# The sample's two token tiles at the end of the output projection, and another order of products in the first two feed-forward units

## The chip, the cores and the metric

The kernel runs on one core of a Trainium2 chip, in one launch. The metric is the device time of an execution in microseconds (us). A core has five engines, each with an instruction queue of its own that is worked through in order: PE (TensorE, the matrix products; PEld are its weight loads), DVE (VectorE), ACT (ScalarE), POOL (GpSimd) and SP (SyncE, which here issues nearly all DMAs). They meet only through semaphores: an instruction waits at the head of its queue until what it reads is written and what it overwrites has been read.

## What is computed

One encoder layer over two inputs: a prompt of 1024 tokens and a sample of 256. A mixer (gated DeltaNet heads and differential attention heads) gives 1024 numbers per token; they go through an output projection, a residual with layer norm, a SwiGLU feed-forward and a second residual with layer norm. Cut to what matters:

```python
def hybrid_mixer(x, w_in, ...):
    h = x @ w_in
    ...
    o_a = gated_deltanet_group(qkv, z, gates, ...)       # 4 heads, scans in both directions
    o_b = diff_attention_group(dq, dk, dv, ...)          # 4 heads, two softmax maps each
    return jnp.concatenate([o_a, o_b], -1) @ w_out       # output projection, 1024 x 1024

def swiglu(x, w_gate_up, w_down):
    gate, up = jnp.split(x @ w_gate_up, 2, axis=-1)      # 2 x 2816 columns
    return (jax.nn.silu(gate) * up) @ w_down

x = layer_norm(ALPHA * x + hybrid_mixer(x, ...), ln1_g, ln1_b)
x = layer_norm(ALPHA * x + swiglu(x, w_gate_up, w_down), ln2_g, ln2_b)
```

The same layer is applied to both inputs. All is float32.

## The kernel before

A product of two float32 matrices is made from three products: each operand is split into a high part (a cast, on ACT) and a low part (operand minus high part, on DVE or POOL), and high by low, low by high and high by high are summed in PSUM. A split thus costs one ACT and one DVE or POOL instruction, and needs two buffers.

The tokens lie in ten tiles of 128: tiles 0 to 7 are the prompt, tiles 8 and 9 the sample. The program has five stages, of which the middle ones matter here.

- **phase_b** (L1068): attention and scans. Attention takes one prompt head, then the sample's heads, then the other three prompt heads (ORDER), so the sample's mixer output is in memory (tensor oT of the sample) long before the prompt's. For the last prompt head attn_finish works through a chain: ACT copies and squares the last block (tiles ao, asq, ass), POOL and DVE make the inverse root (rs_r, rs_t), DVE scales ao, PE transposes it (tile rb_ps), ACT writes tile oT (L889), SP stores it to the tensor oT (L892). Meanwhile load_wout brings the output weights in eight pieces (worw) and splits them (woh on ACT, L1154; wol on DVE, L1155).
- **phase_c** (L1159): output projection and first layer norm, a tile of 128 tokens at a time, in the order of the loop at L1189. Per tile: SP loads oraw from oT (all eight heads of these tokens, L1192) and the residual input xt (L1194), ACT and POOL split oraw into oh and ol, PE does 2 times 24 matmuls of 128x512 into om_ps, DVE adds the residual (L1206), layer_norm (L1122) runs on DVE with a POOL step, two DMAs store the result to x1s (L1143). One tile later, PE transposes it (x_ps, L1174), and ACT and DVE split it: tiles 0 to 3 into B00 and B10, tiles 4 to 7 into Braw and B11, the sample's into xs.
- **x_sums** (L1224): adds and subtracts whole blocks of the transposed prompt (a Strassen scheme: seven block products in place of eight) into T1 to T4, 40 DVE instructions and 16 ACT casts. Its temporaries t come from the pool `post`, of 11 buffers, which also gives p, u and others to the units. This pool lies in memory that phase_c has used before, so its first tile waits for all that still reads or writes there.
- **sweep_up** (L1270): the gate and up products of the feed-forward in 22 units. A unit splits blocks A11, A12, A21, A22 of the weights (pool `sp`, 7 buffers) and makes: gx_ps from B00 with A11, copied to p (L1310), and then onto the same bank B10 with A12; gs_ps, the sample's four products, from xs; gy_ps and gz_ps from T1 to T4 and B11. B10 can be added only when p has been copied. The first two units are generators run in alternation, so that their first parts stand ahead of their Strassen parts.

Nothing in the source fixes the order across engines beyond this: a scheduler reorders each engine's instructions when the program is built, from its own timing model, and picks pool buffers. The order built is the order in which the chip runs them.

Of the kernel before, what the change touches and what calls it, by code (L numbers as in the profile page):

```python
# [1158 lines left out]
def phase_c(k):  # L1159


    nc, tc, V, A = k.nc, k.tc, k.nc.vector, k.nc.scalar
    with ExitStack() as es:
        pool = lambda name, bufs: es.enter_context(tc.tile_pool(name=name, bufs=bufs, side="right"))
        op, cp = pool("c_o", 2), pool("c_x", 3)
        sm, gp = pool("c_s", 2), pool("c_gb", 1)
        gb = [gp.tile([P, DM], F32, name="ln1_" + n) for n in "gb"]

        def transposes(t, xt):
            lo = (t % 4) * P  # L1170
            for b in range(2):
                ps = k.pt.tile([P, 512], F32, tag="tp", name="x1_ps")
                for i in range(4):
                    nc.tensor.transpose(ps[:, i * P:(i + 1) * P], xt[:, (4 * b + i) * P:(4 * b + i + 1) * P], k.ident)  # L1174
                pv = ps.rearrange("p (a b) -> p a b", a=4)
                if t >= 8:
                    h, l = [x[:, 4 * b:4 * b + 4, lo:lo + P] for x in k.xs]
                elif t < 4:
                    h, l = [x[:, :, lo:lo + P] for x in k.B[b, 0]]
                else:  # L1180
                    A.copy(k.Braw[b][:, :, lo:lo + P], pv)
                    if b == 0:
                        continue
                    h, l = [x[:, :, lo:lo + P] for x in k.B[1, 1]]
                A.copy(h, pv)
                V.tensor_tensor(out=l, in0=pv, in1=f32(h), op=ALU.subtract)

        pend = []
        for t in (8, 9, 0, 1, 2, 3, 4, 5, 6, 7):  # L1189
            si, c = (1, t) if t < 8 else (0, t - 8)  # L1190
            raw = op.tile([P, KT, P], F32, tag="oraw", name="oraw")
            nc.sync.dma_start(out=raw, in_=k.S.oT[si].rearrange("k p n -> p k n")[:, :, c * P:(c + 1) * P])  # L1192
            xt = cp.tile([P, DM], F32, tag="xt", name="xt")
            nc.sync.dma_start(out=xt, in_=k.x[si][c * P:(c + 1) * P, :])  # L1194
            if t == 8:
                ln_load(k, k.ln1_g, k.ln1_b, gb)
            if t == 2:
                k.raws = [pair_raw(k, 0), pair_raw(k, 1)]
            oh = op.tile([P, KT, P], F32R, tag="oh", name="oh")
            ol = op.tile([P, KT, P], F32R, tag="ol", name="ol")  # L1200
            split_w(k, raw, oh, ol)
            for o in (0, 512):
                ps = k.pm.tile([P, 512], F32, tag="mm", name="om_ps")
                mm3(nc, ps, lambda i: oh[:, i, :], lambda i: ol[:, i, :],
                    lambda i: k.woh[:, i, o:o + 512], lambda i: k.wol[:, i, o:o + 512], KT)
                V.scalar_tensor_tensor(out=xt[:, o:o + 512], in0=xt[:, o:o + 512], scalar=ALPHA, in1=ps,  # L1206
                                       op0=ALU.mult, op1=ALU.add)
            layer_norm(k, xt, gb, sm, k.S.x1[t])
            pend.append((t, xt))
            if len(pend) > LAG:  # L1210
                transposes(*pend.pop(0))
        for p in pend:
            transposes(*p)
# [46 lines left out]
def mm7(nc, ps, s, t, n, start, stop=True, again=False):  # L1260


    seq = [(s[0], t[1], i) for i in range(n)] + [(s[0], t[0], i) for i in range(n)] + [(s[1], t[0], i) for i in range(n)]
    for j, (a, b, i) in enumerate(seq):
        m = nc.tensor.matmul(ps, lhsT=a(i), rhs=b(i), start=start and j == 0, stop=stop and j == len(seq) - 1,  # L1265
                             skip_group_check=again)
    return m


def sweep_up(k, T, release):  # L1270
# [7 lines left out]
    def split(src):  # L1278
        hi = k.sp.tile([P, 4, P], F32R, tag="sp", name="sph")
        lo = k.sp.tile([P, 4, P], F32R, tag="sp", name="spl")  # L1280
        A.copy(hi, src)  # L1281
        V.tensor_tensor(out=lo, in0=src, in1=f32(hi), op=ALU.subtract)  # L1282
        return part(hi), part(lo)
# [11 lines left out]
    X = {}  # L1295
# [5 lines left out]
    def unit(u):  # L1301

        R = k.raws.pop(0)
        A11, A12, A21, A22 = [R[:, 4 * kh:4 * kh + 4, P * f:P * f + P] for f in range(2) for kh in range(2)]
        px = k.pm.tile([P, 512], F32, tag="mm", name="gx_ps")
        pq = k.pt.tile([P, 512], F32, tag="tp", name="gs_ps")
        p1, u2, u3 = post("p1"), post("u2"), post("u3")
        a = split(A11)
        mm7(nc, px, a, X["11"], 4, True)
        A.copy(p1, px)  # L1310
        mm7(nc, pq[:, 0:256], a, S[0], 4, True, False)
        a = split(A12)
        done = mm7(nc, pq[:, 0:256], a, S[1], 4, False)
        mm7(nc, px, a, X["21"], 4, False, again=True)
        a = split(A21)
        with tc.issue_after(done.ins):
            mm7(nc, pq[:, 256:512], a, S[0], 4, True, False)
        a = split(A22)
        mm7(nc, pq[:, 256:512], a, S[1], 4, False)
        if u < 2:  # L1320
            yield
            a = split(A22)
        py = k.pt.tile([P, 512], F32, tag="tp", name="gy_ps")
        pz = k.pm.tile([P, 512], F32, tag="mm", name="gz_ps")
        if u + 2 < NU:
            k.raws.append(pair_raw(k, u + 2))
        s1 = tmp(A21, A22, ALU.add)
        s2 = tmp(s1, A11, ALU.subtract)
        mm7(nc, py, split(s2), X["T2"], 4, True)
        tt(u2, py, p1, ALU.add)  # L1330
        s3 = tmp(A11, A21, ALU.subtract)
        mm7(nc, py, split(s3), X["T3"], 4, False, again=True)
        tt(u3, py, p1, ALU.add)
        mm7(nc, pz, split(s1), X["T1"], 4, True)
        tt(u3, pz, u3, ALU.add)
        mm7(nc, py, a, X["T4"], 4, False, again=True)
        tt(p1, py, p1, ALU.add)
        s4 = tmp(A12, s2, ALU.subtract)
        a = split(s4)
        if u == NU - 1:  # L1340
            release()
        mm7(nc, pz, a, X["22"], 4, False, again=True)
        tt(u2, pz, u2, ALU.add)
        if u % 2 == 0:
            c11 = post("sg")
            A.activation(c11, px, AF.Silu)
            for x in (u3, p1, u2):
                A.activation(x, x, AF.Silu)
            sq = post("sgs")
            A.activation(sq, pq, AF.Silu)  # L1350
            gate[u] = (c11, u2, p1, u3, sq)
        else:
            finish(u // 2, px, pq, (u2, p1, u3), *gate.pop(u - 1))
# [38 lines left out]
        nc.sync.dma_start(out=k.S.t[p], in_=W.rearrange("p t o f -> p (t o f)"))  # L1392

    pair = [unit(0), unit(1)]
    for g in pair:
        next(g)
    for g in pair:
        for _ in g:
# [211 lines left out]
```

## Time and profile before

| what | value |
|---|---|
| time, median of 3 runs | 1822.12 us (1816.02 to 1822.93) |
| the profiled execution's own time | 1819.94 us |
| span of that execution in the trace | 1818.2 us |
| PE busy / PEld busy | 94% / 82% of the span |
| DVE / ACT / POOL busy | 69% / 41% / 20% of the span |

The trace is of one execution. Times in it count from the span's start; 1.74 us of the execution's time lie outside the span. A row of the timeline gives start, length, engine, source line and what is written from what; matmuls overlap, so a row's length runs past the next row's start, and the distance of the starts is what a group costs. Figures in brackets are the engine's idle time ahead of the row and what ended it. In a row of stretches, each engine has its busy time and, in parentheses, its instructions; after the engines stand PEclk (the clock granted to PE, as a share of full speed: 1.00 is 2.4 GHz, 0.50 is 1.2 GHz), the DMA engines' busy share and GB/s.

### The profile page before, as it was taken

To read this page: it belongs to the slowest core of one execution; us is meant where nothing else is said; L and a number is where in the kernel's file an instruction comes from. 1 tells how busy PE (TensorE), PEld (TensorE's weight loads), DVE (VectorE), ACT (ScalarE), POOL (GpSimd) and SP (SyncE) were. 2 spreads that over 40 slices of the span, in tenths; PEclk is the share of its full clock that TensorE was granted. 3 is DMA by queue.
4 is the path that set the end of the run, shared out by engine and by line. 5 is a ranking of instruction groups with operands and counts; after the bars stand their busy time and mean duration, and the time that the engine had idled before them with its cause. 6 is when DMAs were issued, how large, how long until landed. Compare 5 with 4: busy or idle time off the path is not lost.

```text
span 1818.2 us, 27292 instructions
## 1 busy us (share of the span) xinstructions
PE 1716.0 (94%) x10210; PEld 1486.5 (82%) x10210; DVE 1256.7 (69%) x2092; ACT 747.9 (41%) x1372; POOL 354.7 (20%) x291
## 2 busy tenths in 40 slices
PE   8999889998897899999998899999999999999998
PEld 8988778787785898788887688888888887888886
DVE  4256799998784468977666866566666665666696
ACT  4145564443324767877112432222222222543330
POOL 1013334344314444732330000000000000000011
PEclk9999999998896999999999899999999999999999
DMA  7124444556654987534530433343444332975551
GB/s 234 38 56 119 116 130 134 159 159 190 180 164 104 305 241 219 177 115 162 187 118 35 155 118 123 128 137 127 144 143 144 124 111 96 390 268 176 174 165 70
DMA packets 252035, 279.03 MB, mean 153 GB/s; under 512 B 47217, under 2 KB 196607, under 8 KB 250495
## 3 DMA queue, kind: packets, MB, share of 16 engines
q1 hardware_dynamic: 241999, 265.19, 46.5%
q10 hardware_dynamic: 9904, 12.10, 2.0%
q8 instruction: 80, 1.31, 0.3%
q14 instruction: 52, 0.43, 0.1%
HBM read 183.80 MB, written 93.43 MB: 152 GB/s over the span
## 4 chain that ended last, share of the span: by engine, by line
PE 51%; DVE 3%; DMA 1%; ACT 1%; issue 1%; POOL 0%; POOLq 0%; DVEq 0%; SPq 0%
PE dn_ps L1453 14%; PE gy_ps L1265 10%; PE gx_ps L1265 6%; PE gs_ps L1265 6%; PE gz_ps L1265 6%; PE om_ps L172 6%; PE o_ps L867 1%; DVE t L1236 1%; DVE spl L1282 0%; PE x_ps L1174 0%; ACT ap L831 0%; PE tt_ps L854 0%; PE s_ps L827 0%; DMA wdraw<-in_w_down_dram 0%; PE s_ps L828 0%
## 5 line engine op out<-in xcount | busy, mean ns | idle before, releaser
L308 POOL TENSOR_TENSOR rs_r<-lva,mhalf 128x1 f32<-128x1 f32 x20 | 29.5, 1474 | 854.0 <-DVE lva L1131 835.6
L1281 ACT CAST sph<-wraw 128x512 fp32r<-128x512 f32 x90 | 55.9, 623 | 195.3 <-PE gy_ps L1265 133.3
L172 PE MATMUL dps<-xl,whi 128*128 128x512 f32 (+1 forms) x552 | 125.3, 368 | 7.3 <-ACT st L677 7.3
L172 PE MATMUL dps<-xh,whi 128*128 128x512 f32 (+1 forms) x552 | 123.5, 366 | 0.0
L172 PE MATMUL dps<-xh,wlo 128*128 128x512 f32 (+1 forms) x552 | 122.9, 363 | 0.0
L1281 ACT CAST sph<-wsum 128x512 fp32r<-128x512 f32 x88 | 54.7, 622 | 163.2 <-PE gy_ps L1265 59.8
L172 PEld LDWEIGHTS dps<-xl,whi 128*128 128x128 f32 x552 | 96.3, 197 | 23.6 <-ACT st L677 8.3
L327 DVE SCALAR_TENSOR_TENSOR c<-pad,cw,c 128x1024 f32<-128x1024 f32 (+1 forms) x96 | 89.7, 967 | 28.9 <-ACT c L325 28.5
L1453 PE MATMUL dn_ps<-tth,ssh 128*128 128x512 f32 x280 | 108.9, 389 | 0.0
L1453 PE MATMUL dn_ps<-ttl,ssh 128*128 128x512 f32 x280 | 108.8, 389 | 0.0
L1453 PE MATMUL dn_ps<-tth,ssl 128*128 128x512 f32 x280 | 108.1, 389 | 0.0
L172 PEld LDWEIGHTS dps<-xh,whi 128*128 128x128 f32 x552 | 95.9, 197 | 14.9
L172 PEld LDWEIGHTS dps<-xh,wlo 128*128 128x128 f32 x552 | 94.4, 194 | 14.5
L829 DVE TENSOR_REDUCE ast<-s_ps 128x1 f32<-128x1024 f32 (+1 forms) x80 | 83.6, 1057 | 29.0 <-PE s_ps L828 25.5
L1282 DVE TENSOR_TENSOR spl<-wsum,sph 128x512 fp32r<-128x512 f32 x88 | 60.6, 689 | 49.2 <-issue 22.9
L831 ACT ACTIVATE ap<-s_ps,ast 128x1024 f32<-128x1024 f32 (+1 forms) x80 | 80.1, 1003 | 22.5 <-DVE ast L829 19.7
L1282 DVE TENSOR_TENSOR spl<-wraw,sph 128x512 fp32r<-128x512 f32 x90 | 61.8, 686 | 38.8 <-PE gs_ps L1265 25.2
L1444 ACT CAST ssh<-sraw 128x640 fp32r<-128x640 f32 x77 | 55.9, 727 | 48.4 <-PE dn_ps L1453 36.9
L843 POOL TENSOR_TENSOR ap<-ap,ap 128x512 f32<-128x512 f32 (+2 forms) x60 | 63.3, 1074 | 60.2 <-ACT ap L840 26.4
L1445 DVE TENSOR_TENSOR ssl<-sraw,ssh 128x640 fp32r<-128x640 f32 x77 | 63.0, 820 | 16.7 <-ACT ssh L1444 13.2
L827 PE MATMUL s_ps<-akl,aq 128*128 128x512 f32 (+1 forms) x144 | 64.2, 447 | 8.2 <-ACT ap L831 8.0
L867 PE MATMUL o_ps<-av,tt 128*128 128x128 f32 x544 | 66.3, 280 | 0.0
(363 smaller groups left out, 4431.2 us busy)
## 6 DMA issues: line engine op xcount, KB each, us to landing
ld<-rec SPq DMA_DIRECT2D x160, 192.0 KB, 4.0
sraw<-hs SPq DMA_DIRECT2D x77, 320.0 KB, 4.4
wraw<-in_w_gate_up_dram SPq DMA_DIRECT2D x22, 1024.0 KB, 5.4
wraw<-in_w_in_dram SPq DMA_DIRECT2D x24, 512.0 KB, 4.0
wdraw<-in_w_down_dram SPq DMA_DIRECT2D x11, 1024.0 KB, 4.9
ws<-wdraw SPq DMA_DIRECT2D x11, 1024.0 KB, 3.9
traw<-ws SPq DMA_DIRECT2D x44, 256.0 KB, 4.7
araw<-dqk SPq DMA_DIRECT2D x40, 256.0 KB, 5.4
```

Source lines behind the costliest of these rows:

```text
L172: nc.tensor.matmul(out, lhsT=a(i), rhs=b(i), start=start and j == 0, stop=stop and j == len(seq) - 1)
L327: V.scalar_tensor_tensor(out=out, in0=pad[:, so + w:so + w + n], scalar=k.cw[:, w * 12 + ti:w * 12 + ti + 1], in1=out, op0=ALU.mult, op1=A ...
L827: nc.tensor.matmul(ps[:, o:o + w], lhsT=a.q[m][:, qs], rhs=a.kl[m][:, k0 + o:k0 + o + w], start=True, stop=False)
L829: V.tensor_reduce(out=st[:, m:m + 1], in_=ps, op=ALU.max, axis=AX.X, negate=True)
L831: A.activation(p, ps, AF.Exp, bias=st[:, m:m + 1], accum_out=a.s0[:, i:i + 1] if m == 0 else st[:, 2:3])
L843: nc.gpsimd.tensor_tensor(out=pr[0][:, c], in0=pr[0][:, c], in1=pr[1][:, c], op=ALU.add)
L867: nc.tensor.matmul(ps[:, j * P:(j + 1) * P], lhsT=tt[:, i, j * P:(j + 1) * P], rhs=a.v[:, v0 + i, :], start=i == 0, stop=i == NT[a.si] - 1)
L1265: m = nc.tensor.matmul(ps, lhsT=a(i), rhs=b(i), start=start and j == 0, stop=stop and j == len(seq) - 1, skip_group_check=again)
L1281: A.copy(hi, src)
L1282: V.tensor_tensor(out=lo, in0=src, in1=f32(hi), op=ALU.subtract)
L1445: V.tensor_tensor(out=lo, in0=src, in1=f32(hi), op=ALU.subtract)
L1453: nc.tensor.matmul(ps, lhsT=a[:, c], rhs=b, start=z == 0 and j == 0, stop=z == NPR - 1 and j == 2)
```

## The change

Three edits, no work added to the products themselves. The loop of phase_c takes the prompt's tiles 0 to 7 first and the sample's tiles 8 and 9 last. The first two units make the B10 product right after B00 and before the sample's four products; since the sample's products then come in a later step of the generator, A11 and A12 are split a second time for them (two more splits in each of the two units). And both generators are advanced twice in alternation before they are run out, so that the source has the B parts of both units, then the sample's parts of both.

```diff
--- before.py
+++ after.py
@@ -1186,13 +1186,13 @@
                 V.tensor_tensor(out=l, in0=pv, in1=f32(h), op=ALU.subtract)
 
         pend = []
-        for t in (8, 9, 0, 1, 2, 3, 4, 5, 6, 7):
+        for t in (0, 1, 2, 3, 4, 5, 6, 7, 8, 9):
             si, c = (1, t) if t < 8 else (0, t - 8)
             raw = op.tile([P, KT, P], F32, tag="oraw", name="oraw")
             nc.sync.dma_start(out=raw, in_=k.S.oT[si].rearrange("k p n -> p k n")[:, :, c * P:(c + 1) * P])
             xt = cp.tile([P, DM], F32, tag="xt", name="xt")
             nc.sync.dma_start(out=xt, in_=k.x[si][c * P:(c + 1) * P, :])
-            if t == 8:
+            if t == 0:
                 ln_load(k, k.ln1_g, k.ln1_b, gb)
             if t == 2:
                 k.raws = [pair_raw(k, 0), pair_raw(k, 1)]
@@ -1308,10 +1308,15 @@
         a = split(A11)
         mm7(nc, px, a, X["11"], 4, True)
         A.copy(p1, px)
+        if u < 2:
+            mm7(nc, px, split(A12), X["21"], 4, False, again=True)
+            yield
+            a = split(A11)
         mm7(nc, pq[:, 0:256], a, S[0], 4, True, False)
         a = split(A12)
         done = mm7(nc, pq[:, 0:256], a, S[1], 4, False)
-        mm7(nc, px, a, X["21"], 4, False, again=True)
+        if u >= 2:
+            mm7(nc, px, a, X["21"], 4, False, again=True)
         a = split(A21)
         with tc.issue_after(done.ins):
             mm7(nc, pq[:, 256:512], a, S[0], 4, True, False)
@@ -1392,7 +1397,7 @@
         nc.sync.dma_start(out=k.S.t[p], in_=W.rearrange("p t o f -> p (t o f)"))
 
     pair = [unit(0), unit(1)]
-    for g in pair:
+    for g in pair + pair:
         next(g)
     for g in pair:
         for _ in g:
```

What the scheduler makes of it on PE, at the end of attention. Here tt_ps and o_ps are attention's last transposes and products, rb_ps the transposes of the last head's output, om_ps the output projection. Before:

```order
L854 MATMUL tt_ps<-identr,ap_8517 128x128 x8
L867 MATMUL o_ps<-av,tt 128x128 x8
L172 MATMUL om_ps<-wol,oh 128x512 x2
L867 MATMUL o_ps<-av,tt 128x128 x8
L172 MATMUL om_ps<-wol,oh 128x512 x27
L172 MATMUL om_ps<-woh,ol 128x512 x8
L172 MATMUL om_ps<-woh,oh 128x512 x7
L888 MATMUL rb_ps<-identr,ao 128x128 x8
L172 MATMUL om_ps<-woh,oh 128x512
```

and now:

```order
L854 MATMUL tt_ps<-identr,ap_8517 128x128 x8
L867 MATMUL o_ps<-av,tt 128x128 x16
L888 MATMUL rb_ps<-identr,ao 128x128 x8
L172 MATMUL om_ps<-wol,oh 128x512 x24
L172 MATMUL om_ps<-woh,ol 128x512 x8
```

The 96 matmuls of the sample's two tiles no longer stand around the last head's transposes; the first output projection on PE is now that of prompt tile 0, behind rb_ps.

On DVE, from the last layer norm of phase_c to the first instruction of x_sums (tile t; spl is the low part of a weight split, B11l and xsl those of the last transposed tile). Before:

```order
L1129 BN_AGGR lmv<-lst 128x2
L1186 TENSOR_TENSOR B11l<-x_ps,B11h 128x4x128
L1282 TENSOR_TENSOR spl<-wraw,sph 128x512
L1289 TENSOR_TENSOR wsum<-wraw,wsum 128x512
L1131 TENSOR_SCALAR lva<-lmv 128x1
L1132 SCALAR_TENSOR_TENSOR xt<-xt,lmv,ln_g 128x1024
L309 SCALAR_TENSOR_TENSOR rs_t<-rs_r 128x1
L310 TENSOR_TENSOR rs_t<-rs_t,lva 128x1
L311 SCALAR_TENSOR_TENSOR rs_r<-rs_t,rs_r 128x1
L1142 SCALAR_TENSOR_TENSOR xt<-xt,rs_r,ln_b 128x512 x2
L1236 TENSOR_TENSOR t_9661<-Braw_8688,B00h 128x512
```

and now:

```order
L1129 BN_AGGR lmv<-lst 128x2
L1282 TENSOR_TENSOR spl<-wraw,sph 128x512 x2
L1289 TENSOR_TENSOR wsum<-wraw,wsum 128x512
L1131 TENSOR_SCALAR lva<-lmv 128x1
L1132 SCALAR_TENSOR_TENSOR xt<-xt,lmv,ln_g 128x1024
L1282 TENSOR_TENSOR spl<-wraw,sph 128x512
L309 SCALAR_TENSOR_TENSOR rs_t<-rs_r 128x1
L310 TENSOR_TENSOR rs_t<-rs_t,lva 128x1
L311 SCALAR_TENSOR_TENSOR rs_r<-rs_t,rs_r 128x1
L1142 SCALAR_TENSOR_TENSOR xt<-xt,rs_r,ln_b 128x512 x2
L1186 TENSOR_TENSOR xsl<-x_ps,xsh 128x4x128
L1236 TENSOR_TENSOR t_9661<-Braw_8688,B00h 128x512
```

The first t stands behind the last tile's layer norm in both; more weight splits stand ahead of it now.

On PE in the first two units, from the last out-projection transposes but one to the sample's first products, before:

```order
L1174 MATMUL x_ps<-identr,xt 128x128 x8
L1265 MATMUL gx_ps<-B00l,sph 128x512 x4
L1265 MATMUL gx_ps<-B00h,sph 128x512 x4
L1265 MATMUL gx_ps<-B00h,spl 128x512 x4
L1174 MATMUL x_ps<-identr,xt 128x128 x8
L1265 MATMUL gs_ps<-xsl,sph 128x256 x4
```

and now, down to the first B10 product (the rows left out are the rest of the sample's products):

```order
L1265 MATMUL gx_ps<-B00l,sph 128x512 x4
L1265 MATMUL gx_ps<-B00h,sph 128x512 x4
L1265 MATMUL gx_ps<-B00h,spl 128x512 x4
L1174 MATMUL x_ps<-identr,xt 128x128 x8
L1265 MATMUL gs_ps<-xsl,sph 128x256 x4
L1265 MATMUL gs_ps<-xsh,sph 128x256 x4
...
L1265 MATMUL gs_ps<-xsh,spl 128x256 x4
L1265 MATMUL gy_ps<-T2l,sph 128x512 x3
L1265 MATMUL gx_ps<-B10l,sph 128x512 x4
```

Two groups of twelve B00 matmuls (one shown) now stand ahead of the last transposes instead of one. The B10 products stand where they stood before: behind all of the sample's products and three matmuls of gy_ps.

## Rows read from the trace of the kernel before

**Rows 1.** The page of the profile: the span, and each engine's busy time, its share of the span and its instructions.

```profile
span 1818.2 us, 27292 instructions
...
PE 1716.0 (94%) x10210; PEld 1486.5 (82%) x10210; DVE 1256.7 (69%) x2092; ACT 747.9 (41%) x1372; POOL 354.7 (20%) x291
```

**Rows 2.** Timeline of PE from the last attention products to the first output projection of a prompt tile: start us, length us, engine, line, operation.

```profile
854.24 0.70 PE L172 MATMUL om_ps<-wol,oh 128*128 128x512 f32 x2
854.78 1.95 PE L867 MATMUL o_ps<-av,tt 128*128 128x128 f32 x16
856.48 6.39 PE L172 MATMUL om_ps<-wol,oh 128*128 128x512 f32 x27
...
866.11 1.04 PE L888 MATMUL rb_ps<-identr,ao 128*128 128x128 f32 x8
...
878.82 2.21 PE L172 MATMUL om_ps<-wol,oh 128*128 128x512 f32 x9
```

**Rows 3.** Timeline of the other engines over the same stretch: start us, length us, engine, line, operation; SPq are DMA issues on SP.

```profile
858.39 0.16 DVE L878 SCALAR_TENSOR_TENSOR ass<-ass,as 128x8 f32<-128x8 f32 x1
858.63 1.64 POOL L308 TENSOR_TENSOR rs_r<-ass,mhalf 128x8 f32<-128x8 f32 x1 [1.54 <-DVE ass L878]
858.69 1.05 ACT L1154 CAST woh<-worw 128x1024 fp32r<-128x1024 f32 x1 [0.54 <-DMA worw<-in_w_out_dram]
859.77 1.23 DVE L1155 TENSOR_TENSOR wol<-worw,woh 128x1024 fp32r<-128x1024 f32 x1 [1.22 <-ACT woh L1154]
...
861.51 1.29 DVE L881 TENSOR_TENSOR ao<-ao,rs_r 128x512 f32<-128x512 f32 x2
...
868.04 0.34 SPq L892 DMA_DIRECT2D oT<-oT  x1
...
872.41 0.99 SPq L1192 DMA_DIRECT2D oraw<-oT  x2
...
876.74 1.05 ACT L162 CAST oh<-oraw 128x1024 fp32r<-128x1024 f32 x1 [8.72 <-DMA oraw<-oT]
```

**Rows 4.** Source line L892, the stores of tile oT: the issues, and the time from issue to landing over all of them.

```profile
L892 SPq DMA_DIRECT2D oT<-oT x4: 320/332/505, 675.7 to 868.0; - x4
...
DMA to landing us min/median/max: 3.0/4.3/6.2
```

**Rows 5.** Stretches of the span, all engines: start:end, length, then busy us and instructions of PE, PEld, DVE, ACT, POOL, then PEclk, DMA share and GB/s.

```profile
851.00:973.00 122.00, 122.00 (x586) 102.60 (x585) 76.90 (x133) 24.29 (x41) 38.98 (x20) 0.99 0.45 147
977.00:982.50 5.50, 0.00 (x0) 0.00 (x0) 4.96 (x12) 0.00 (x0) 1.51 (x1) 0.82 0.00 0
982.50:987.00 4.50, 4.46 (x21) 4.46 (x22) 0.65 (x1) 1.66 (x3) 0.00 (x0) 0.50 0.34 120
1001.00:1009.00 8.00, 2.27 (x7) 1.12 (x7) 7.96 (x14) 4.25 (x8) 0.00 (x0) 0.71 0.39 131
1009.00:1014.50 5.50, 5.31 (x13) 4.15 (x14) 5.50 (x10) 3.67 (x7) 0.00 (x0) 0.50 0.18 57
1014.50:1025.00 10.50, 10.46 (x46) 8.31 (x44) 8.31 (x15) 2.50 (x5) 0.00 (x0) 0.99 0.51 171
```

**Rows 6.** The chain of work that ended last, from the last two tiles of the output projection to the first B10 product: start us, us, what.

```profile
950.59 10.90 PE om_ps L172 x48
...
962.36 10.91 PE om_ps L172 x48
...
983.18 4.33 DMA x1s<-xt
...
1002.46 0.60 DVE T4l L1242
...
1008.65 0.49 ACT p L1310
```

**Rows 7.** Timeline of PE from the end of the output projection to the first B10 product.

```profile
975.90 1.07 PE L1265 MATMUL gx_ps<-B00h,spl 128*128 128x512 f32 x4
982.54 1.97 PE L1174 MATMUL x_ps<-identr,xt 128*128 128x128 f32 x8 [5.57 <-DVE xt L1142]
984.16 1.20 PE L1265 MATMUL gs_ps<-xsl,sph 128*128 128x256 f32 x4
...
1001.31 0.74 PE L1265 MATMUL gs_ps<-xsh,spl 128*128 128x256 f32 x4 [1.74 <-DVE spl L1282]
1003.08 0.73 PE L1265 MATMUL gy_ps<-T2l,sph 128*128 128x512 f32 x2 [1.03 <-ACT sph L1281]
1006.12 0.80 PE L1265 MATMUL gy_ps<-T2l,sph 128*128 128x512 f32 x1 [2.31 <-DVE T2l L1242]
1009.19 2.07 PE L1265 MATMUL gx_ps<-B10l,sph 128*128 128x512 f32 x4 [2.27 <-ACT p L1310]
```

**Rows 8.** Timeline of DVE over the same stretch.

```profile
973.30 0.69 DVE L1206 SCALAR_TENSOR_TENSOR xt<-xt,om_ps 128x512 f32<-128x512 f32 x1 [4.03 <-PE om_ps L172]
...
981.15 0.16 DVE L309 SCALAR_TENSOR_TENSOR rs_t<-rs_r 128x1 f32<-128x1 f32 x1 [0.44 <-POOL rs_r L308]
...
987.92 0.69 DVE L1236 TENSOR_TENSOR t<-Braw,B00h 128x512 f32<-128x512 f32 x1 [4.77 <-ACT sph L1281]
...
1007.31 0.69 DVE L1236 TENSOR_TENSOR t<-Braw,t 128x512 f32<-128x512 f32 x1
```

## The prediction

> **What bounds the kernel now.** I read the page first: PE is busy for 94% of the span and no other engine passes 69% [rows 1], so an edit pays only where it fills a gap of PE, and costs where it opens one. The diff touches the stretch from the end of attention to the second unit, and the order built for after differs from before's only there, so I read that stretch engine by engine.
>
> At the end of attention PE has no gap: busy for 122.00 of the 122.00 us from 851 to 973 [rows 5]. That is not for want of a wait. The last head's chain runs through it: ass ends on DVE at 858.55, POOL's rs_r takes 1.64, ao is scaled at 861.51, the transposes rb_ps stand at 866.11, oT's store is issued at 868.04, the load of tile 0 that needs it at 872.41, its cast at 876.74, and tile 0 begins on PE at 878.82 [rows 2, 3]. All the while PE works on the sample's 96 om_ps matmuls, whose input has long been in memory. They are the cover of this chain.
>
> Behind the output projection PE waits often: 5.57 us for the last layer norm (DVE tile xt), 1.74 and 1.03 for weight splits, 2.31 for T2l, 2.27 for p; in sum 12.92 [rows 7]. There DVE is the bound: busy for 7.96 of the 8.00 us ahead of 1009 while PE has 2.27 [rows 5]. The chain of waits says so too: last om_ps, layer norm, store and reload x1s, T sums, p, then B10 at 1009.19 [rows 6, 7].
>
> **Term 1: the cover that goes.** With the prompt first, the first om_ps on PE is tile 0's, and it needs all eight heads of those tokens, so the load behind the last store. Nothing else is ready. The work removed from here is done later, at 10.90 and 10.91 us a tile [rows 6], so it costs nothing by itself: the loss is the gap.
> Where the chain then runs: o_ps no longer has two om_ps matmuls between its halves, which saves about 0.5, and ends near 855.9 (16 rows begin at 854.78, the next work at 856.48, with 0.54 from the two matmuls at 854.24) [rows 2]. ass is kept at 858.4: in after the last woh cast and wol stand ahead of it on ACT and DVE, which in before start at 858.69 and 859.77 because ACT waits for worw [rows 3]; but two oraw loads of the sample no longer stand ahead of worw on SP, so worw should land earlier. From 858.4: +0.24 to rs_r, +1.64, then DVE from 860.9 to 861.6 for the small steps and the first half of ao as in before (861.51 is where ao begins, 0.64 a half). rb_ps can begin at 861.6 instead of 866.11, since no om_ps stands ahead of it on PE. To the store 1.93 (866.11 to 868.04), to the load's issue 4.37 (to 872.41: the load waits on SP for the store's landing), to the cast 4.33 (to 876.74), the cast 1.05 [rows 2, 3]: PE begins tile 0 at 873.3.
> After a wait of 5.57 us PE ran at a granted clock of 0.50, that is 1.2 GHz, for the 4.50 us from 982.5 [rows 5]. Here the wait is some 10 us, so I take the same: 4.5 us at half speed, 2.2 lost. The eight tiles took 973.30 - 878.82 = 94.5 [rows 2, 8], with eight groups of transposes among them, as now among ten; two tiles more are 21.8. End of the output projection: 873.3 + 2.2 + 94.5 + 21.8 = 991.8 against 973.3, **+18.5**.
> Bounds. Low: the store lands in 3.0, the least that L892 shows (median 4.3, so my 4.37) [rows 4], 1.4 less, and the clock stays up, 2.2 less: 14.9. High: worw lands as in before, so ass waits behind wol until 859.77 + 1.23 = 861.0, +2.6, and the store lands in 6.2, the most shown, +1.8: 22.9. I stay in the middle since all its steps have a row of the same instruction.
>
> The Trainium skill says in "TensorE: Matmul & The Clock Gate", section "What's actually happening", that the throttled state is the default and that activity releases it. Without that half-speed stretch the sum would be 2.2 us less, which the range holds already; the 0.50 behind 5.57 idle us [rows 5] agrees with the rule.
>
> **Term 2: the seam behind the output projection.** The source puts B10 ahead of the sample's products; the order built does not. B10 still stands behind all gs_ps and three gy_ps matmuls, since p's buffer comes from post, as do the t, and the first t still stands behind the last layer norm on DVE and waits for x1s to land (983.18, 4.33; t at 987.92) [rows 6, 8]. So neither edit shortens the chain; what counts is what was added to DVE.
> Ahead of the landing: one xsl more (net of what moved) and one spl more, 0.60 each by T4l, the same form of work [rows 6]; a third spl falls into DVE's wait for POOL of 0.44 ahead of rs_t [rows 8] and leaves 0.16. Together about 1.4. Behind the landing: 35 DVE instructions instead of 33 up to the last t, 1.2. The first of the sample's splits now needs a buffer of sp while only three of seven are free, because the sample's products can begin only when the last xsl is there; I take one stall of 1.0, as the 1.03 wait for sph [rows 7]. Sum 1.4 + 1.2 + 1.0 = **+3.6**.
> Bounds. Low: no stall (-1.0), and the 5.50 us from 1009, in which PE ran at 0.50 [rows 5], run at full clock since the sample's products now lie nearer (-2.7): -0.1. High: all four split steps behind it stall as well, +4.0: 7.6. I stay near the middle: nothing in the order takes the T sums off DVE, so PE will be as idle ahead of B10 as it was.
> At no cost: the extra splits' casts, since ACT has 4.25 of 8.00 us in that stretch [rows 5]; unit 1's twelve B00 matmuls (1.07 for four [rows 7]) that now fill part of the 5.57 gap, which gain nothing either, since the wait for DVE ends last there. If DVE's cover went, they would be worth some 2.7. The change of loop moves the loads of later tiles only behind each other on SP; they come a tile ahead, and nothing waited for them from 878.82 to 973 [rows 5].
>
> **Sum.** 1819.94 + 18.5 + 3.6 = 1842.0 on the profiled execution's own time. That one lies 2.2 us below the median of the runs shown (1822.12), and I split the difference: **1843**. The bounds give 1819.94 + 14.9 - 0.1 = 1834.7 and 1819.94 + 22.9 + 7.6 = 1850.4.
>
> **Rivals.**
> A, the gap is paid back behind (not slower). The prompt's tiles are done two tiles earlier; if the T sums ran on DVE under the sample's 96 matmuls (DVE is busy for only 76.90 of 122 us there [rows 5]), the waits of 12.9 us and both stretches at half clock (2.25 + 2.7) would go: 17.9 back, so 1819.94 + 18.5 - 17.9 = 1820.5, within 0.5%. What decides is where the first t stands and what it waits for. Against it: the built order has it behind the last layer norm, and its memory is phase_c's. Chance 0.07.
> The Trainium skill's "Perfetto Trace Analysis", section "Optimization Strategy", says that kernels with several regimes may gain by interleaving them. This kernel already does so at the end of attention, and by that rule the change exchanges one such place for another; the trace shows only the first of them to be a cover [rows 5].
> B, starved splits (slower still). With three sp buffers free the eight sample splits each wait for a release, 1.0 each: 8.0 in place of 1.0, 1819.94 + 18.5 + 2.6 + 8.0 = 1849, with its bounds up to 1853. Against it: once the sample's products flow, each releases a buffer. Chance 0.08.
> C, the cover goes but costs less, with some of the seam paid: tile 0's chain at its low bound and half of A's waits (6.5) gone, 1819.94 + 14.9 - 6.5 = 1828. Against it as in A. Chance 0.06.
> That B10 does not move is no rival but part of the forecast.
>
> **How the numbers follow.** The forecast has 0.79. A measurement of this kernel tells about 0.5% from no change, 9.1 us: the limits are 1813.0 and 1831.2. Faster: 0.02, for a cause I do not see. Same: A and C partly, 0.10. Slower: the rest, 0.88. The range goes from 1831, to take in some of C, to 1851, the upper bound; it leaves out A, most of C and the end of B, some 0.17.
>
> **What would show it.** In the profile of after: PE idle for 10 to 11 us between rb_ps and the first om_ps, which starts at about 873; PEclk 0.50 at the start of the output projection; its last om_ps ending near 992; no om_ps before rb_ps. Then the first t right behind the landing of x1s, DVE without gaps to the p copy, and B10 some 39.5 us behind the end of the output projection where it was 35.9 (973.30 to 1009.19). Past B10 the two profiles should run in step. I would be wrong in term 1 if om_ps began before 870 or after 877, in term 2 if t began before the last layer norm, or if B10 stood ahead of gs_ps.

## The result and the profile after

The change makes the kernel slower: 1840.70 us median of six runs (1838.24 to 1845.93) against 1818.55 us for the kernel before (1811.16 to 1822.93), ratio 1.0115 with the 95% interval 1.0093 to 1.0136. That is 16.9 to 24.7 us more. The profiled execution took 1840.32 us, 20.4 us more than that of before.

The first view has rows of PE's timeline at the end of attention, which answers to [rows 2]; the last group but one of 32 o_ps products (846.72) is the last landmark that both kernels have in the same order.

```profile
846.72 3.74 PE L867 MATMUL o_ps<-av,tt 128*128 128x128 f32 x32
853.31 1.94 PE L854 MATMUL tt_ps<-identr,ap 128*128 128x128 f32 x8 [2.86 <-DVE as L877]
855.04 4.34 PE L867 MATMUL o_ps<-av,tt 128*128 128x128 f32 x32
864.43 1.97 PE L888 MATMUL rb_ps<-identr,ao 128*128 128x128 f32 x8 [5.04 <-DVE ao L881]
876.82 7.32 PE L172 MATMUL om_ps<-wol,oh 128*128 128x512 f32 x24 [10.43 <-ACT oh L162]
```

The same landmark in the kernel before, PE's timeline:

```profile
843.69 3.74 PE L867 MATMUL o_ps<-av,tt 128*128 128x128 f32 x32
```

So this execution came 3.03 us late to the landmark (846.72 against 843.69) over work in the same order: that belongs to the execution, not to the change; the runs below do the same work up to there and reach it between 843.69 and 850.28. Everything below is counted from it. Where PE had no gap behind its wait for tile as (2.57 us before, 2.86 now), it now waits 5.04 us ahead of rb_ps and 10.43 us ahead of tile 0.

Rows of the other engines over the same stretch, beside [rows 3]:

```profile
861.18 0.16 DVE L878 SCALAR_TENSOR_TENSOR ass<-ass,as 128x8 f32<-128x8 f32 x1
861.41 1.63 POOL L308 TENSOR_TENSOR rs_r<-ass,mhalf 128x8 f32<-128x8 f32 x1 [29.36 <-DVE ass L878]
863.68 1.29 DVE L881 TENSOR_TENSOR ao<-ao,rs_r 128x512 f32<-128x512 f32 x2
867.15 0.34 SPq L892 DMA_DIRECT2D oT<-oT  x1
871.46 8.14 SPq L1192 DMA_DIRECT2D oraw<-oT  x3
875.73 1.04 ACT L162 CAST oh<-oraw 128x1024 fp32r<-128x1024 f32 x1 [8.60 <-DMA oraw<-oT]
```

It is the chain of [rows 3], step by step, without the work that lay over it: store to load 4.31 us (4.37 before), load to cast 4.27 (4.33).

Stretches of after: the start of the output projection, the way to the first B10 product, and that product; the columns are those of [rows 5], PE, PEld, DVE, ACT, POOL, then PEclk, DMA share and GB/s:

```profile
876.80:881.30 4.50, 4.48 (x13) 3.58 (x14) 0.00 (x0) 1.04 (x1) 4.45 (x2) 0.62 0.17 46
996.00:1031.40 35.40, 22.96 (x130) 18.32 (x128) 33.03 (x59) 15.92 (x29) 2.12 (x1) 0.94 0.09 32
1031.00:1036.50 5.50, 5.08 (x12) 4.01 (x13) 5.50 (x10) 3.90 (x7) 0.00 (x0) 0.50 0.46 143
```

PE starts the output projection at a granted clock of 0.62 over 4.50 us, where 0.50 was forecast, and B10 still runs at 1.2 GHz (0.50). From 996 to B10 DVE is busy for 33.03 of 35.40 us, PE for 22.96.

The seam behind the output projection, rows of PE's timeline beside [rows 7]:

```profile
1005.77 1.76 PE L1174 MATMUL x_ps<-identr,xt 128*128 128x128 f32 x8 [3.64 <-DVE xt L1142]
1012.10 0.74 PE L1265 MATMUL gs_ps<-xsh,spl 128*128 128x256 f32 x4 [0.71 <-DVE spl L1282]
1015.11 0.74 PE L1265 MATMUL gs_ps<-xsh,spl 128*128 128x256 f32 x4 [1.21 <-DVE spl L1282]
1021.73 0.74 PE L1265 MATMUL gs_ps<-xsh,spl 128*128 128x256 f32 x4 [1.32 <-DVE spl L1282]
1031.42 2.07 PE L1265 MATMUL gx_ps<-B10l,sph 128*128 128x512 f32 x4 [3.16 <-ACT p L1310]
```

and its chain of waits beside [rows 6]:

```profile
983.79 10.91 PE om_ps L172 x48
994.73 0.69 DVE xt L1206
...
1004.97 1.43 DVE xt L1142 x2
1006.41 2.03 DMA x1s<-xt
1008.82 0.69 DVE t L1236
```

The output projection ends at 994.73; the first t still follows the last layer norm and the store, and B10 stands where it stood, 36.69 us behind the end of the output projection (35.89 before).

The bill, with the start of unit 0's first silu (ACT row sg<-gx_ps, 1026.92 before, 1049.32 after) as a third mark:

| stretch | before | after | difference |
|---|---|---|---|
| start to the landmark | 843.69 | 846.72 | +3.03 |
| landmark to the end of the output projection | 129.61 | 148.01 | **+18.40** |
| from there to B10 | 35.89 | 36.69 | +0.80 |
| B10 to the first silu | 17.73 | 17.90 | +0.17 |
| silu to the end of the span | 791.28 | 789.18 | -2.10 |
| span | 1818.2 | 1838.5 | +20.3 |

The first and the last line lie where the two orders are the same. Part of the last is a half-clock stretch at the start of the down sweep, which the execution of before has and that of after has not:

```profile
1545.00:1558.00 13.00, 12.09 (x46) 9.85 (x47) 12.85 (x24) 9.02 (x14) 0.00 (x0) 0.87 1.03 381
```

and after:

```profile
1567.00:1580.00 13.00, 12.15 (x53) 10.06 (x54) 13.00 (x23) 8.52 (x14) 0.00 (x0) 1.00 1.01 364
```

### The profile page after: what moved, and what is told of

Its sections match the earlier page's. It is cut to its first block, busy times and chain, and to the rows that moved or that the text cites. A ratio compares the mean times of both kernels' runs of the same rounds, so it can differ in the third digit from the quotient of the medians.

```text
span 1838.5 us, 27312 instructions
## 1 busy us (share of the span) xinstructions
PE 1716.2 (93%) x10210; PEld 1483.4 (81%) x10210; DVE 1266.5 (69%) x2096; ACT 750.2 (41%) x1376; POOL 353.7 (19%) x291
## 3 DMA queue, kind: packets, MB, share of 16 engines
q8 instruction: 80, 1.31, 0.3%
## 4 chain that ended last, share of the span: by engine, by line
PE 50%; DVE 2%; issue 2%; DMA 1%; ACT 1%; POOL 0%; POOLq 0%; DVEq 0%; SPq 0%; ACTq 0%
PE dn_ps L1458 14%; PE gy_ps L1265 9%; PE gx_ps L1265 6%; PE gs_ps L1265 6%; PE gz_ps L1265 6%; PE om_ps L172 6%; PE o_ps L867 1%; DVE t L1236 0%; DVE spl L1282 0%; PE x_ps L1174 0%; POOL rs_r L308 0%; DMA wdraw<-in_w_down_dram 0%; PE s_ps L827 0%; DMA oT<-oT 0%; PE s_ps L828 0%
```

## Experiments

The theory: the loss is the cover that left the last head's chain, and nothing else of weight. The rivals: the new order of the units costs it; the prompt-first order costs by loads or late memory; half-speed clock does it. For each run the table gives the ratio to before with its 95% interval, the distance from the landmark (o_ps x32) to the end of the output projection (DVE's last xt<-xt,om_ps), as its difference from the 129.61 us of before, and the distance from there to the first silu. The ratios come from all executions of a run, the distances from the one that was profiled.

| run | ratio (95%) | landmark to end of projection, against before | from there to the first silu |
|---|---|---|---|
| before | 1 | 843.69 to 973.30: 129.61 | 53.62 |
| after | 1.0115 (1.0093 to 1.0136) | 846.72 to 994.73: +18.40 | 54.59 |
| e1_loop_only | 1.0098 (1.0079 to 1.0117) | 847.52 to 995.98: +18.85 | 53.18 |
| e2_units_only | 1.0003 (0.9990 to 1.0017) | 848.31 to 978.09: +0.17 | 53.56 |
| e3_one_first | 1.0053 (1.0039 to 1.0067) | 845.36 to 985.59: +10.62 | 52.04 |
| e4_split_load | 1.0001 (0.9986 to 1.0015) | 844.63 to 976.35: +2.11 | 53.22 |
| e5_pools | 1.0115 (1.0094 to 1.0136) | 845.55 to 994.79: +19.63 | 54.13 |
| e6_split_pools_own_p | 1.0005 (0.9989 to 1.0020) | 845.28 to 978.05: +3.16 | 49.57 |
| e7_before_loop_own_p | 1.0023 (1.0005 to 1.0042) | 850.28 to 982.48: +2.59 | 52.11 |
| e8_warm | 1.0122 (1.0089 to 1.0154) | 850.00 to 997.75: +18.14 | 54.51 |
| e9_own_p_pad | 0.9985 (0.9971 to 0.9999) | 849.67 to 980.76: +1.48 | 50.83 |
| e10_own_p_pad_pool | 1.0018 (1.0004 to 1.0032) | 844.60 to 975.80: +1.59 | 54.06 |
| e11_warm_80 | 1.0094 (1.0063 to 1.0125) | 845.77 to 992.90: +17.52 | 53.00 |
| e12_before_t_lows_pool | 1.0027 (1.0012 to 1.0042) | 849.01 to 978.42: -0.20 | 56.30 |

**The two halves of the change.** The loop order alone:

```diff
-        for t in (8, 9, 0, 1, 2, 3, 4, 5, 6, 7):
+        for t in (0, 1, 2, 3, 4, 5, 6, 7, 8, 9):
-            if t == 8:
+            if t == 0:
```

> Only the loop order of the change: prompt tiles 0 to 7 first, the sample's 8 and 9 last, the units as before. Theory (the loss is the cover that left the last head's chain): PE again idle for some 15 us around rb_ps and the first output projection, 18.4 us later at the end of the output projection than before; slower than before by 17 to 21 us, about as the whole change. Rival (the loss sits in the new order of the first units, the loop order is free): within 5 us of before.

The units' edits alone, with the loop of before:

> Only the edits of the first two units (B10 ahead in the source, two more splits in each), the loop order as before. Theory: PE stays busy through the last head's chain, and the seam behind the output projection is 0 to 2 us longer by the added splits on DVE; within 4 us of before. Rival (the units are the loss): 15 us slower or more.

The loop order alone costs 1.0098 and +18.85 us at the projection; the units' edits alone 1.0003 and +0.17. The whole loss is in the loop order.

**Half of the cover.** As the change, with `for t in (8, 0, 1, 2, 3, 4, 5, 6, 7, 9)`.

> The change, but with one of the sample's tiles in front again (8, 0 to 7, 9): half of the cover. Theory (the gap is the last head's chain less the ready work): one tile of 10.9 us lies in the gap, which falls from 15.5 us to about 5, with some 2 us at half clock behind it; 7 to 9 us slower than before, about 11 to 13 faster than the change. Rival (any prompt tile that follows the last head costs the same wait, however much work lies ahead): as slow as the change, 18 us or more. Second rival (half-speed clock and order effects, not the amount of cover): between 0 and 3 us slower than before.

PE's timeline around tile 0:

```profile
869.14 0.72 PE L172 MATMUL om_ps<-woh,oh 128*128 128x512 f32 x2
874.85 1.94 PE L1174 MATMUL x_ps<-identr,xt 128*128 128x128 f32 x8 [5.00 <-DVE xt L1142]
878.28 8.50 PE L172 MATMUL om_ps<-wol,oh 128*128 128x512 f32 x24 [1.49 <-ACT oh L162]
```

One tile in front, 10.9 us of work, takes the loss at the projection from 18.40 to 10.62, by 7.78. In the times the loss is 9.7 us (7.1 to 12.2, of 1822.86), where 7 to 9 was expected. Two things were larger than expected in the trace: PE is idle there for 7.64 us in all (5.00 and 1.49 above, 0.66 and 0.49 for wol ahead of them) and not for some 5, and the first 24 matmuls of tile 0 take 8.50 us against 7.32 in the change.

**Cover of another kind.** The change, with the last head's part of tiles 0 and 1 apart:

```diff
-            nc.sync.dma_start(out=raw, in_=k.S.oT[si].rearrange(...)[:, :, c * P:(c + 1) * P])
+            src = k.S.oT[si].rearrange("k p n -> p k n")[:, :, c * P:(c + 1) * P]
+            cuts = (0, 7, 8) if t < 2 else (0, 8)
+            for a, b in zip(cuts, cuts[1:]):
+                nc.sync.dma_start(out=raw[:, a:b], in_=src[:, a:b])
...
+            for a, b in zip(cuts, cuts[1:]):
+                split_w(k, raw[:, a:b], oh[:, a:b], ol[:, a:b])
...
+            for a, b in zip(cuts, cuts[1:]):
+                for o in (0, 512):
+                    mm3(nc, pss[o], ..., b - a, start=a == 0, again=a > 0)
```

> The change, but tiles 0 and 1 load, split and multiply the last head's part apart from the other seven heads: 84 of their 96 matmuls no longer need the last head's output. Same products, other order of sums. Theory (the wait is for the last head's store and reload alone): these 84 matmuls (19 us) fill the gap of 15.5 us; end of the output projection within 2 us of before, the time within 4 us of before and 16 to 20 us under the change. Rival (the prompt-first order costs by its loads, or memory that comes free later): at most 5 us under the change.

```profile
866.75 1.03 PE L889 MATMUL rb_ps<-identr,ao 128*128 128x128 f32 x8
867.53 1.18 PE L172 MATMUL om_ps<-woh,ol 128*128 128x512 f32 x4
...
881.71 6.89 PE L172 MATMUL om_ps<-wol,oh 128*128 128x512 f32 x29 [1.64 <-ACT oh L162]
```

With the prompt still first, PE's one wait there is 1.64 us in this timeline, and the time is that of before (1.0001, from 2.6 us less to 2.7 us more). So the prompt-first order as such costs nothing that these runs can tell; what costs is that all 48 matmuls of its first tile stand behind one head's store and reload.

**The clock.** The change, with transposes of the last head's output added behind rb_ps (result unused), 56 and then 80:

```diff
+    if a.si == 1 and a.h == 3:
+        ps = k.pt.tile([P, 512], F32, tag="tp", name="warm_ps")
+        for i in range(56):
+            nc.tensor.transpose(ps[:, (i % 4) * P:(i % 4 + 1) * P], oT[:, (i % 8) * P:(i % 8 + 1) * P], k.ident)
```

> The change, with 56 transposes of the last head's output added on PE behind rb_ps (their result is not used), so that PE works in the gap. They end before tile 0's operands are there. Theory (tile 0 begins at half clock because PE was idle): the granted clock in the first 5 us of the output projection is 1.00 and its first 24 matmuls take 5.5 us where they took 7.3; the end of the output projection is some 2 us earlier than in the change, counted from attention's last common products. Rival (the slow start has another cause, as operands that come late): the 24 matmuls take 7 us or more again.

> The change with 80 added transposes instead of 56, so that PE's work lasts until about the first output projection and leaves it idle for less than 1 us ahead of it. Theory (PE's clock falls in idle time, and with 56 the last 2.5 idle us were enough): granted clock 1.00 over the first 5 us of the output projection, its first 24 matmuls 5.5 to 5.8 us. Rival (transposes do not keep the clock, whatever their number): half clock for some 3 us again.

With 56, PE was idle for 2.50 us ahead of tile 0. The stretch from there:

```profile
880.00:885.00 5.00, 4.97 (x16) 3.98 (x17) 0.00 (x0) 1.04 (x1) 4.72 (x2) 0.69 0.27 77
```

With 80, idle for 0.40 us, the stretch of the same kind:

```profile
876.60:881.10 4.50, 4.50 (x20) 3.72 (x21) 0.00 (x0) 1.05 (x1) 4.48 (x2) 1.00 0.16 44
```

The first did not come out as expected: PE's granted clock was 1.00 under the last transposes (873.0 to 877.5), and 0.50 behind the 2.50 idle us (880.0 to 882.0). The second did: 1.00, and from the first om_ps (876.60) to the end of the projection 116.30 us against 117.91 in the change (876.82 to 994.73). Between these two executions the half-speed start is worth 1.6 us. It is not a gain in time: the added work let tile 0 begin 0.73 us later behind the landmark, and 1.0094 can't be told from 1.0115.

**Paying back in the seam.** The memory of the output projection in another order, so that the T sums' buffers lie over operands that come free with the last om_ps:

```diff
-        op, cp = pool("c_o", 2), pool("c_x", 3)
-        sm, gp = pool("c_s", 2), pool("c_gb", 1)
+        cp, sm, gp = pool("c_x", 3), pool("c_s", 2), pool("c_gb", 1)
+        op = pool("c_o", 2)
...
-    for n in (1, 2, 3, 4):
+    for n in (1, 2, 4, 3):
```

> The change, but the output projection's memory is laid out in another order, so that the buffers of the T sums lie over operands that come free with its last matmul, and no longer over the rows and norm constants that the last layer norm and the store to x1s still use. In the order built the first t now stands right behind the last om_ps, 13 us earlier. Theory (behind the output projection DVE is the bound and part of its time is the wait for the store to land): PE's waits from the end of the output projection to the second unit's sums, some 12 us in the change, fall by 3 to 6; 3 to 6 us faster than the change, so still 13 to 18 slower than before. Rival (DVE has as much to do in any order): within 1 us of the change. Rival A of the prediction, taken at its word (T sums early pay the whole loss back): within 3 us of before.

PE's timeline, at the last transposes:

```profile
1011.58 1.76 PE L1174 MATMUL x_ps<-identr,xt 128*128 128x128 f32 x7 [8.26 <-DVE xt L1142]
```

All engines of e5_pools behind the last om_ps, in the columns of [rows 5]:

```profile
994.80:1031.00 36.20, 21.91 (x109) 18.66 (x108) 35.77 (x63) 16.55 (x31) 2.72 (x1) 0.76 0.06 17
```

The first t now stood right behind the last om_ps on DVE (994.79 and 995.39), and nothing was won: the last layer norm came that much later (PE waited 8.26 us for it, 3.64 in the change), and the distance to the first silu fell by 0.46 only. With the wait for the store gone, DVE is busy for 35.77 of 36.20 us, so its work still sets the end. B10 came earlier, 32.78 us behind the last om_ps (1027.57) where it was 36.69, and that won nothing either.

Then with the split load and two buffers of its own for p (`d_pp`, `d_post` from 11 to 10), in the loop order of the change and in that of before:

> The change with three edits: the last head's part of tiles 0 and 1 apart, the T sums' memory as in the run with the other layout, and two buffers of their own for p of the first two units (the shared ones fall from 11 to 10). The order built now has both units' B10 ahead of the last transposes, as the source asks. Theory: the cover is back (0 to 2 us from before) and the 5.4 us of B10 products fill the wait for the last layer norm, with less half-speed clock behind; 4 to 9 us faster than before. Rival (DVE is the bound up to the T sums, so products moved forward only lengthen the later waits): within 2 us of before.

> As the run before it, but with the loop order of before (sample first) and no split load: units' edits, memory layout, buffers of their own for p. Theory (the loop order is not needed for the early B10, since B10 needs only tiles 0 to 3): also 4 to 9 us faster than before, within 3 us of the run before it. Rival (the early T sums under the sample's tiles are what pays): 4 us or more slower than the run before it.

Now B10 does stand in the wait for the last layer norm, and the distance to the first silu falls to 49.57, 4.05 less than before; with the loop of before only to 52.11. There the first t stands 14.00 us behind the last om_ps (996.48, 0.61 in e6) and waits last for ACT's write of Braw (1.28 us), which with the loop of before is filled last, by tile 7; e7 has no split load either. But no time was won (1.0005 and 1.0023), where 4 to 9 us were expected: the projection had become slower. Its matmuls in this layout, rows of PE's timeline of e5_pools, then the same two groups in after:

```profile
973.28 2.02 PE L172 MATMUL om_ps<-woh,ol 128*128 128x512 f32 x8
975.14 2.02 PE L172 MATMUL om_ps<-woh,oh 128*128 128x512 f32 x8
```

```profile
973.68 1.98 PE L172 MATMUL om_ps<-woh,ol 128*128 128x512 f32 x8
975.50 1.98 PE L172 MATMUL om_ps<-woh,oh 128*128 128x512 f32 x8
```

By the starts, eight take 1.86 us in place of 1.81 or 1.82, and a tile with its transposes 12.02 in place of 11.78 (982.57 to 994.59 against 982.75 to 994.53), some 2.4 us over ten tiles. With 640 unused bytes ahead of the operands,

```diff
+        sm.tile([P, 80], F32, tag="pad", name="pad")
         op = pool("c_o", 2)
```

> The run with split load, other layout and own buffers for p, and 640 bytes of unused memory ahead of oraw, oh and ol, which puts them back to the distance from woh and wol, modulo 1024 bytes, that they had in before. Nothing else differs, the order on PE is the same. Theory (in the other layout each om_ps matmul takes 0.232 us in place of 0.227 because of where its operands lie): 0.227 again, a tile 11.77 us and not 12.02, 2.5 us less over ten tiles; 2 to 5 us faster than before. Rival (the slower matmuls come from other traffic, DVE or DMA, at that time): 0.232 again, and the same time as without the 640 bytes.

```profile
971.49 1.98 PE L172 MATMUL om_ps<-woh,ol 128*128 128x512 f32 x8
973.30 1.98 PE L172 MATMUL om_ps<-woh,oh 128*128 128x512 f32 x8
```

the 1.81 are back, in PE's timeline of e9_own_p_pad, and this version is the only one whose interval lies under both kernels: 0.9985 (0.9971 to 0.9999), 2.7 us of 1822.73, 0.2 to 5.3. Of the twelve runs it is the only one that is faster than before, and by the edge of its interval; its profile shows less, 1.31 us from the landmark to the first silu (181.92 against 183.23). What the 640 bytes are worth in time stays open: against e6 the projection is 1.68 us shorter and the seam behind it 1.26 us longer, and the two ratios overlap.

**Is DVE the bound?** Two runs move the low parts of T1 and T4 to POOL: e10 in the version with the 640 bytes (e9), e12 in the kernel before.

```diff
-        V.tensor_tensor(out=l, in0=t[n, c], in1=f32(h), op=ALU.subtract)
+        (k.nc.gpsimd if n in (1, 4) else V).tensor_tensor(out=l, in0=t[n, c], in1=f32(h), op=ALU.subtract)
```

> As the run before it, with the low parts of T1 and T4 (8 of the 40 DVE instructions of the T sums) on POOL, which is idle there. Theory (DVE is the bound from the end of the output projection to the first sums of unit 0): 8 times 0.60 = 4.8 us less on DVE, 3 to 5 us of them won; 5 to 9 us faster than before. Rival (POOL's slower instruction, some 1.2 us for this size by its ol rows, comes to stand in the chain instead): within 2 us of the run before it.

> The kernel before, with the low parts of T1 and T4 on POOL instead of DVE (8 instructions of 0.60 us). Theory (DVE sets the distance from the end of the output projection to B10): the 35.9 us from there to B10 fall by 2 to 4 us, since 5 to 7 of the 8 stand ahead of the last t; 2 to 4 us faster than before. Rival (the wait for the store and the sample's splits set it): distance and time unchanged within 1 us.

Both became slower than what they started from (1.0018 against 0.9985, and 1.0027 against 1), the distance to the first silu by 3.23 and 2.68 us. DVE's timeline of e10_own_p_pad_pool:

```profile
997.99 0.69 DVE L1246 TENSOR_TENSOR t<-Braw,B00h 128x512 f32<-128x512 f32 x1
998.60 1.78 DVE L1252 TENSOR_TENSOR T2l<-t,T2h 128x512 fp32r<-128x512 f32 x1
1000.30 1.77 DVE L1246 TENSOR_TENSOR t<-t,B10l 128x512 f32<-128x512 f32 x1
1001.99 1.77 DVE L1292 TENSOR_TENSOR spl<-wraw,sph 128x512 fp32r<-128x512 f32 x1
```

and POOL's:

```profile
998.10 1.73 POOL L1252 TENSOR_TENSOR T1l<-t,T1h 128x512 fp32r<-128x512 f32 x1 [9.06 <-DVE t L1246]
999.79 1.74 POOL L1252 TENSOR_TENSOR T4l<-t,T4h 128x512 fp32r<-128x512 f32 x1
1001.48 1.73 POOL L1252 TENSOR_TENSOR T1l<-t,T1h 128x512 fp32r<-128x512 f32 x1
```

While POOL works, DVE does one instruction per POOL instruction, 1.77 us instead of 0.68. So these two runs did not lighten DVE: from the last om_ps to the first silu it is busy for 52.44 us in e10 and 48.58 in e9, for 49.25 in e12 and 45.54 in before. The question rests on e5, where DVE has no time left, and no run with less work on DVE was made.

## Why the prediction was right

It gave 1843 (1831 to 1851), slower at 0.88; measured were 1840.7. Term 1, which is nearly all of the loss, is right in its steps. That the total came so close has luck in it: the profiled execution lay 1.7 us under its forecast (1840.32 against 1842.0), which is -0.10 in term 1, -2.80 in term 2, +0.17 up to the first silu, +3.03 ahead of the landmark and -2.10 at the end, and the last two were not forecast.

- **Term 1**, forecast +18.5, measured +18.40. Moved back by 3.03 us, the steps of the chain came at 858.15 (ass, forecast 858.4), 861.40 (rb_ps, 861.6), 864.12 (store, 863.5), 868.43 (load), 872.70 (cast) and 873.79 (tile 0, 873.3), and the projection ended at 991.70 (991.8). The last woh cast, moved back likewise, began at 855.93 (858.69 before), so worw landed earlier, as assumed. The store came 0.6 later than forecast, since rb_ps itself ran at 1.2 GHz (1.97 us for its eight, 1.04 before). The clock's part was 1.6 (e11) and not 2.2; that and the later start nearly cancel. e1 to e4 show the mechanism: the loss comes with the loop order, goes down with the work in front, and goes away when other work is made ready.
- **Term 2**, forecast +3.6, measured +0.80 (B10 36.69 us behind the projection, 39.5 forecast): inside its bounds but mis-sized in three places. Up to the store's issue it is +1.80 (983.18 - 973.30 = 9.88 against 1006.41 - 994.73 = 11.68; forecast 1.4): the third spl did not fall into DVE's wait for POOL, since POOL's rs_r took 2.12 us in place of 1.51 and DVE again waited 0.44 behind it. Behind the first t it is +1.33 (21.27 against 22.60; forecast 2.2, of which 1.0 for a stall that did not come). Between the two it is -2.33, which the sum lacked: t followed the store's issue by 4.74 us before (983.18 to 987.92) and by 2.41 in after (1006.41 to 1008.82). I had carried the 4.33 for the landing over as fixed; in after it is 2.03, and t follows the landing by 0.41 and 0.38. That figure goes with the units' edits, not with the loop: e1, without them, has t 4.62 us behind the issue of its last store (1006.46 to 1011.08), e2, which has them alone, 2.44 (989.18 to 991.62), and e4 2.25 (988.04 to 990.29).

POOL's rs_r of the last layer norm, before and after:

```profile
979.60 1.51 POOL L308 TENSOR_TENSOR rs_r<-lva,mhalf 128x1 f32<-128x1 f32 x1 [14.64 <-DVE lva L1131]
1002.23 2.12 POOL L308 TENSOR_TENSOR rs_r<-lva,mhalf 128x1 f32<-128x1 f32 x1 [15.84 <-DVE lva L1131]
```

What the DMAs moved around the last store, 5.00 us in 40 slices: before (983 to 988), with a packet of instructions in that stretch (its MB, and its share of the 16 engines) and the store's KB and us to landing; then after (1006.4 to 1011.4), where no such packet is:

```profile
GB/s 0 0 115 344 410 377 377 344 410 328 541 311 410 213 17 0 0 0 0 0 0 0 0 16 0 16 0 16 16 16 33 16 0 0 0 0 0 0 0 0
q8 instruction: 1, 0.02, 2.1%
x1s<-xt SPq DMA_DIRECT2D x1, 256.0 KB, 4.3
```

```profile
GB/s 0 213 410 344 426 328 426 344 442 328 459 311 164 0 0 0 0 0 0 0 0 0 0 0 0 0 0 0 0 0 0 0 0 0 0 0 0 0 0 0
x1s<-xt SPq DMA_DIRECT2D x1, 256.0 KB, 2.0
```

In before nearly all of the store is through by 985, and a small rest trickles up to 987. The late landings (4.33 in before, 4.23 in e1, 4.10 in e12) each have a packet of instructions in the same stretch; after, e2 and e4, with 2.0, have none. So the kernel's instructions seem to have been fetched in the store's way, and the units' edits moved the fetch to another place. No run moves the fetch alone, so this cause is argued, not shown.

- **Rival A** (paid back behind) failed as argued: the first t stands behind the last layer norm. The reason given against it, that t's memory is phase_c's, was true and not enough: e5 put that memory over operands that come free with the last om_ps, t began right there, and the time did not move (1.0115). No run put the T sums under the sample's 96 matmuls, so what that would give back is not shown. **Rival B** (splits starved): PE's waits for spl ahead of the sample's products were 0.71, 1.21 and 1.32 us, not eight of 1.0. **Rival C**: the chain did not come out cheaper.
- B10 unmoved was forecast and seen. With the other layout alone (e5) it stood 32.78 us behind the projection, with buffers of its own for p on top of it 5.42 in e6 (983.47) and 5.34 in e7 (987.82); those buffers without the layout were not tried.
- The profiles do run in step past the seam up to the start of the down sweep; the -2.10 there were not foreseen.

## What to carry to other kernels

Work that is ready early is cover, and its worth is the chain that runs under it: before moving it, follow that chain through stores, reloads and queue waits, and price it at its bare length. If an order has to change, make other work ready (here seven heads of eight) before giving the old cover up. An order in the source moves nothing while a buffer pool or a shared engine holds the operand back: look at the order built.

## What the hardware showed that was not expected

- The same 128x512 matmul takes 0.227 or 0.232 us by where oh and ol lie. e6 and e9 differ in the source by the 640 unused bytes alone: a tile with its transposes takes 12.03 us in e6 (965.83 to 977.86) and 11.77 in e9 (968.79 to 980.56). Which distance it takes, and why, was not tried.
- DVE and POOL instructions that both read two operands from memory alternate: 0.68 us becomes 1.77 beside a POOL instruction of 1.73. The Trainium skill has it in "SBUF — State Buffer", section "Who interferes with whom": a DVE instruction with two SBUF inputs contends with a GpSimd instruction that reads SBUF. The rows above agree.
- Behind 56 transposes (7.84 us) and 2.50 idle us PE's granted clock was 0.69 over the next 5 us (e8); behind 80 transposes (10.29 us) and 0.40 idle us it was 1.00 (e11).
- The same 256 KB store landed 4.1 to 4.3 us behind its issue where a packet of instructions was fetched in that stretch (before, e1, e12), and 2.0 us where none was (after, e2, e4). Whether the fetch is the cause was not tested.
